# Ordering the mixers and attentions of a two-layer trunk with busy intervals for ScalarE and VectorE

## The chip, the cores and the metric

The kernel runs on one core of a Trainium2 chip. The metric is the device time of one execution in microseconds (us). The kernel before took 1425.7 us, the median of three runs from 1424.77 to 1426.21.

Five engines work in parallel, each taking its own instructions strictly in order: TensorE (PE in the profile: matmuls; PEld: the loads of their stationary operand), VectorE (DVE), ScalarE (ACT), GpSimd (POOL) and SyncE (SP, which here only issues transfers). An instruction that has to wait holds up all that stand behind it on its engine.

## The reference

A trunk of two layers over 512 positions of width 1024, with a memory of 256 positions, all in float32:

```
x += mixer(rms_norm(x));  x += cross_attention(rms_norm(x), mem);  x += conv_ffn(rms_norm(x))    (twice)
layer 0 mixer: forgetting attention, 8 heads of 64  |  differential attention, 4 heads (2 x 64, values 128)
    fox:   softmax(q k' / 8 + F_q - F_k, causal) v,  F = cumsum(log_sigmoid(gate))
    diff:  (softmax(q1 k1' / 8) - lam * softmax(q2 k2' / 8)) v, then an rms_norm of its own
layer 1 mixer: mLSTM, 4 heads (q, k 128 after a causal convolution, values 256), gated, normalised
conv_ffn: gated, with a depthwise convolution of 3 taps and 2816 hidden columns
```

## The kernel before, in words

**Precision.** Every weight arrives by a transfer of 512 KB that SP issues (`weight`, L325) and is split in two: ScalarE rounds it to the fast matmul type (`wh`, a CAST), VectorE computes the rest (`wl`, a TENSOR_TENSOR). A product is three matmuls: high by high, low by high, high by low (`mm3`, L340 to L342; with tokens on the partitions L402 to L404). So TensorE carries three passes of everything, and a projection of 1024 by 128 columns for 512 positions is 24 matmuls of 512 columns.

**Stages.** Mixer 0 runs from 0 to about 230 us of the span, cross attention 0 to about 375, the FFN of layer 0 to about 720, mixer 1 to about 915, cross attention 1 to about 1080, and the FFN of layer 1 with the final norm to the end. The FFNs are ordered by another scheduler (`Sched`), which the change leaves alone.

**What sets the order.** Mixers and cross attentions are a list of items (`Plan.add`): a piece of TensorE work with a planned duration, what it depends on, a priority, the buffers it takes and frees, and a `chain` of what follows on other engines, such as 0.6 us on D (VectorE) and then 0.52 on A (ScalarE). `Plan.run` walks a planned TensorE clock, and each time takes the item with the best priority that can start now. When it takes an item, the Python function of the item is called, and that writes the instructions of all engines into the program: the order of VectorE's, ScalarE's and GpSimd's instructions follows from the order in which items are taken. Planned times are used for nothing else; on the chip, semaphores decide.

Four banks (`acc`) hold the sums of projections, two banks (`s`) the scores, two (`w`) transposes, weighted values and the like. Helpers record most VectorE and ScalarE instructions under one line, L262.

**Softmax.** A score is two matmuls (L750, L751) into an `s` bank; VectorE adds the bias or mask and takes the minimum in one instruction (CUSTOM_DVE_ANT_0), ScalarE takes the exponential with its sum (ACTIVATE x<-x,sm), VectorE inverts the sum (RECIPROCAL) and scales (TENSOR_SCALAR). Then TensorE transposes (L781), VectorE and ScalarE copy the result out (`pt`), and TensorE multiplies by the values: a weigh (L793 for a differential head, L1008 for a pair of fox heads).

**Roots.** A differential head's rms_norm (`p_far_norm`) goes: TensorE sums squares by columns (L499), VectorE makes `z`, GpSimd takes the power (`y`, L507) and issues two transfers, `roots` out to DRAM (L448) and `hrb` back, spread to all partitions (L452); then VectorE multiplies the head by it (`ta<-ta,warm,hrb`, a SCALAR_TENSOR_TENSOR). There is one `hrb` buffer. The heads of the mLSTM do the same (`num<-num,vec,hrb`).

**Fillers.** In mixer 0 the keys of cross attention 0, `acc<-mem` with 256 columns and 192 matmuls in all, stand at the lowest priority (`p_fill`), and so does the output projection (`p_out`, its weights `wo`). Whatever is free at that moment fills TensorE where the attention has nothing ready.

**mLSTM.** The gates (`p_gate`) go through a long run of small VectorE and ScalarE instructions; `ucols` (L1630) transposes their result back. Meanwhile q and k of the first head are projected, convolved on VectorE (`hs`, `cv`) and ScalarE, and scored (L1721, `s<-q,k`).

## Time and profile before

| | us |
|---|---|
| median of three runs | 1425.7 |
| lowest, highest | 1424.77, 1426.21 |
| the profiled execution's own time | 1423.48 |
| its span in the trace | 1421.7 |
| TensorE busy | 1403.3 (99%) |
| VectorE busy | 1133.5 (80%) |
| ScalarE busy | 823.8 (58%) |
| GpSimd busy | 129.9 (9%) |

The profiled execution is 2.2 us below the median of the runs. Time that the profile calls busy isn't always time at full rate: a matmul of 512 columns lasts 0.38 us in the trace and a new one starts every 0.216 us, so the starts tell more than the shares. The granted clock (PEclk) says for each slice of the span at what part of full speed TensorE's clock ran; 1.00 is full speed.

### The profile page before, as it was taken

The page shows a single profiled execution, that of the slowest core. Times are in us where ns is not written, and L with a number is a line of the kernel's source. Part 1 is how long each engine was busy: PE and PEld are TensorE (multiplying, and loading weights), DVE is VectorE, ACT ScalarE, POOL GpSimd, SP SyncE. Part 2 cuts the span into 40 slices and gives each one's busy share as a digit, 9 for nine tenths or more (in the row PEclk, how much of TensorE's full clock was granted, in tenths as well). Part 3 has the DMA queues.
Part 4 walks back from the last instruction along what each step waited for, and adds up shares of the span by engine and source line. Part 5 has one row for each costly group of instructions (what it writes and reads, how often), then busy time and mean ns, then how long its engine had stood idle before and what let it go on. Part 6 is the DMA issues. An engine that isn't in the chain of part 4 may idle for free.

```text
span 1421.7 us, 22241 instructions
## 1 busy us (share of the span) xinstructions
PE 1403.3 (99%) x8440; PEld 1262.9 (89%) x8440; DVE 1133.5 (80%) x1906; ACT 823.8 (58%) x1382; POOL 129.9 (9%) x189
## 2 busy tenths in 40 slices
PE   9999999999999999999999999999999999999998
PEld 7878788899889999999887788989988999999997
DVE  7778596666689999999768657667667999999984
ACT  7777574444476656566456654445445665656655
POOL 0001240000001111110001210000000111111000
PEclk9999999999999999999999999999999999999999
DMA  5233224323248777773233322323323886777522
GB/s 205 90 108 108 90 79 152 132 76 133 86 150 217 191 180 184 182 182 106 86 105 112 105 95 97 119 92 120 130 74 120 212 202 171 193 179 185 143 77 80
DMA packets 69211, 190.02 MB, mean 134 GB/s; under 512 B 7552, under 2 KB 7552, under 8 KB 69104
## 3 DMA queue, kind: packets, MB, share of 16 engines
q1 hardware_dynamic: 55648, 153.48, 32.3%
q0 software_dynamic: 12448, 34.00, 13.7%
q8 instruction: 66, 1.08, 0.3%
q10 hardware_dynamic: 1008, 1.12, 0.2%
q14 instruction: 41, 0.34, 0.1%
HBM read 186.43 MB, written 2.15 MB: 133 GB/s over the span
## 4 chain that ended last, share of the span: by engine, by line
PE 83%; DVE 8%; ACT 4%; issue 3%; DMA 1%; POOL 1%; SPq 0%; POOLq 0%; DVEq 0%; ACTq 0%
PE acc L340 16%; PE acc L341 16%; PE acc L342 16%; PE w L340 5%; PE w L342 5%; PE w L341 5%; PE s L340 3%; PE s L341 3%; PE s L342 3%; PE acc L402 2%; PE acc L404 2%; PE acc L403 2%; DVE wl L262 2%; DVE x L262 1%; PE w L1765 1%
## 5 line engine op out<-in xcount | busy, mean ns | idle before, releaser
L262 ACT CAST wh<-raw 128x1024 fp32r<-128x1024 f32 (+2 forms) x229 | 235.0, 1027 | 205.6 <-PE acc L341 118.8
L262 DVE TENSOR_TENSOR wl<-raw,wh 128x1024 fp32r<-128x1024 f32 (+2 forms) x229 | 274.2, 1198 | 38.7 <-ACT wh L262 38.2
L340 PE MATMUL acc<-xh,wh 128*128 128x512 f32 (+1 forms) x800 | 278.6, 348 | 0.8 <-ACT v L262 0.8
L341 PE MATMUL acc<-xl,wh 128*128 128x512 f32 (+1 forms) x800 | 274.0, 343 | 0.0
L342 PE MATMUL acc<-xh,wl 128*128 128x512 f32 (+1 forms) x800 | 273.6, 342 | 0.0
L340 PEld LDWEIGHTS acc<-xh,wh 128*128 128x128 f32 x800 | 152.5, 191 | 14.5 <-ACT v L262 1.2
L342 PEld LDWEIGHTS acc<-xh,wl 128*128 128x128 f32 x800 | 152.4, 190 | 13.9
L341 PEld LDWEIGHTS acc<-xl,wh 128*128 128x128 f32 x800 | 152.5, 191 | 13.2
L262 DVE SCALAR_TENSOR_TENSOR c<-hs,vec,c 128x512 f32<-128x512 f32 x176 | 131.8, 749 | 3.8 <-ACT c L262 0.8
L340 PE MATMUL w<-ah,wh 128*128 128x512 f32 x304 | 115.7, 381 | 0.2 <-ACT c L262 0.2
L342 PE MATMUL w<-ah,wl 128*128 128x512 f32 x304 | 115.2, 379 | 0.0
L341 PE MATMUL w<-al,wh 128*128 128x512 f32 x304 | 115.2, 379 | 0.0
L262 ACT ACTIVATE c<-hs,vec 128x512 f32<-128x512 f32 x88 | 70.8, 811 | 9.9 <-DVE hs L262 5.4
L262 ACT CAST ah<-c 128x512 fp32r<-128x512 f32 x44 | 27.2, 619 | 83.8 <-DVE c L262 83.8
L262 DVE TENSOR_TENSOR x<-acc,x 128x512 f32<-128x512 f32 (+1 forms) x43 | 28.1, 653 | 54.2 <-PE acc L342 53.4
L340 PEld LDWEIGHTS w<-ah,wh 128*128 128x128 f32 x304 | 57.6, 190 | 8.0 <-DVE x L262 0.9
L342 PEld LDWEIGHTS w<-ah,wl 128*128 128x128 f32 x304 | 57.5, 189 | 8.1
L341 PEld LDWEIGHTS w<-al,wh 128*128 128x128 f32 x304 | 57.6, 190 | 6.5
L342 PE MATMUL acc<-mem,wl 128*128 128x256 f32 (+1 forms) x192 | 59.9, 312 | 0.0
L340 PE MATMUL acc<-mem,wh 128*128 128x256 f32 (+1 forms) x192 | 59.6, 311 | 0.0
L341 PE MATMUL acc<-mem,wh 128*128 128x256 f32 (+1 forms) x192 | 59.6, 311 | 0.0
L1446 POOL DMA_DIRECT2D sa<-in_up_dram x36 | 30.8, 857 | 290.6 <-DMA sa<-in_up_dram 212.7
(357 smaller groups left out, 3750.5 us busy)
## 6 DMA issues: line engine op xcount, KB each, us to landing
raw<-in_up_dram SPq DMA_DIRECT2D x52, 512.0 KB, 3.7
sa<-in_up_dram SPq DMA_DIRECT2D x36, 512.0 KB, 3.4
sa<-in_up_dram POOLq DMA_DIRECT2D x36, 512.0 KB, 5.9
raw<-in_down_dram SPq DMA_DIRECT2D x32, 512.0 KB, 3.6
ra<-in_up_dram SPq DMA_DIRECT2D x36, 256.0 KB, 4.0
sb<-in_up_dram POOLq DMA_DIRECT2D x36, 256.0 KB, 4.9
raw<-in_xk_dram SPq DMA_DIRECT2D x16, 512.0 KB, 3.2
raw<-in_wo_dram SPq DMA_DIRECT2D x16, 512.0 KB, 3.3
```

The costliest lines, as they stand in the source:

```text
L262: i = issue(*a, **k)
L340: mm(out, wh, xh, start=first, stop=False, skip_group_check=parts)
L341: mm(out, wh, xl, start=False, stop=False, skip_group_check=parts)
L342: mm(out, wl, xh, start=False, stop=last, skip_group_check=parts)
L402: mm(ps, xh[k][:, ts], wh, start=(k == 0), stop=False)
L403: mm(ps, xh[k][:, ts], wl, start=False, stop=False)
L404: mm(ps, xl[k][:, ts], wh, start=False, stop=(k == 7))
L1446: return add("POOL", 0.0029 * cols, lambda: nc.gpsimd.dma_start(out(), src(), accum_op=ALU.add), deps, due, (), (), 6.0)
L1765: nc.tensor.matmul(ps[:, lo:], vv[s][:, c], a[:], start=(s == 0), stop=(s == 3))
```

## The change

No instruction of the computation is added or taken away. What changes is the planner and its numbers, and by them the order of the instructions.

- **Busy intervals.** For A (ScalarE), D (VectorE) and G (GpSimd) the planner kept one time each: when the engine is free. Now it keeps a list of busy intervals, and `place` puts a piece of work into the first gap that holds it. A long chain that waits for something no longer pushes all later work behind it in the plan.
- **Costs.** Planned durations change: ScalarE's 0.52 and 0.5 become 0.6, an exponential 0.4 + 0.45 for 512 columns instead of 0.3 + 0.4, GpSimd's power 1.3 instead of 1.05, and so on. The values' evacuation counts on ScalarE alone (`rest=False`). The gate chain of mixer 1 becomes a delay of 14 us with a load spread over gaps, and the step after it 4.0 instead of 2.7.
- **Banks.** An `acc` bank of a projection is planned free at the end of the first step of its chain (`soon`), the first read, and no longer at the end of all.
- **Holding.** An item that waits for a buffer kept every later item off this buffer; now only if it could start within 2.5 us (`HOLD`).
- **Roots and memory.** `LATE`, the planned time between asking for the roots and using them, is 15 us instead of 12, so the use is written later. The memory's transfers are planned 16 instead of 10 us ahead of use.

```diff
-ROW_DMA, SPREAD_DMA, LATE = 2.7, 6.0, 12.0
+ROW_DMA, SPREAD_DMA, LATE = 2.7, 6.0, 15.0
+HOLD = 2.5
...
+        def place(e, at, d):
+            b = eng[e]
+            while b and b[0][1] < t - 8.0:
+                b.pop(0)
+            n = 0
+            for n, (x, y) in enumerate(b):
+                if at + d <= x:
+                    break
+                at = max(at, y)
+            else:
+                n = len(b)
+            b.insert(n, (at, at + d))
+            return at + d
...
-                held |= set(i.take)
-                if any(len(self.res[r]) < i.take.count(r) for r in i.take):
+                if any(len(res[r]) < i.take.count(r) for r in i.take):
+                    held |= set(i.take)
                     continue
...
+                if at < t + HOLD:
+                    held |= set(i.take)
...
             for e, d in pick.pre:
-                eng[e] = max(eng[e], t - 4.0) + d
+                place(e, t - 4.0, d)
             t += pick.dur
             u = t + (0.1 if pick.chain else 0.0)
+            clear = None
             for e, d in pick.chain:
-                if e == "-":
-                    u += d
-                    continue
-                u = max(u, eng[e]) + d
-                eng[e] = u
-                u += 0.06
+                u = u + d if e == "-" else place(e, u, d) + 0.1
+                clear = clear or u
             for e, d in pick.load:
-                eng[e] = max(eng[e], t) + d
+                while d > 0.0:
+                    place(e, t, min(d, 0.6))
+                    d -= 0.6
...
-                    self.banks[pick.st["banks"].pop(0)] = u
+                    banks[owned.setdefault(id(pick.st), list(pick.st.get("banks", ()))).pop(0)] = clear if pick.soon else u
...
-            last = pl.add(lambda c=c: load(c), 0, (), 0, after=at + step * c - 10.0, order=[*order, last])
+            last = pl.add(lambda c=c: load(c), 0, (), 0, after=at + step * c - 16.0, order=[*order, last])
...
-            g = pl.add(lambda: None, 0, [g], 1, chain=(("A", 1.0), ("D", 7.0), ("A", 0.5)))
-            gk = pl.add(lambda: None, 0, [g], 2, chain=(("-", ROW_DMA),))
+            g = pl.add(lambda: None, 0, [g], 1, chain=(("-", 14.0),), load=(("A", 5.0), ("D", 7.0)))
+            gk = pl.add(lambda: None, 0, [g], 2, chain=(("-", 4.0),), load=(("A", 2.4), ("D", 1.2)))
```

In the rows below, numbers behind a name tell tiles of one kind apart; they differ between the two kernels. L262 before is L295 after, and all later lines move by 33.

**A root's use, mixer 0, third differential head.** On TensorE before, the sums of squares of that head stand here, between two projections of the fox part, in front of the last transposes of the head behind (`w_1489`) and two scores:

```order
L340 MATMUL acc_276_1409<-xh_32_234,wh_1404 128x512
L341 MATMUL acc_276_1409<-xl_33_235,wh_1404 128x512
L342 MATMUL acc_276_1409<-xh_32_234,wl_1405 128x512
L499 MATMUL s_1480<-ones_82,tb_1422 128x2 x4
L781 MATMUL w_1489<-ident,x_141 128x128 x4
L750 MATMUL s_1500<-ka_257_1331,qa_249_1285 128x384
```

On VectorE before, the use of its root (`hrb_1568`) stands in the middle of the softmax of the next scores; `x_138` and `x_142` are scores, `pt` copies of transposes:

```order
L262 TENSOR_SCALAR x_140<-x_140,sm_1507 128x384
L262 COPY pt_1370<-w_1543 128x128
L262 ISA x_142,sm_1557<-s_1550,tb_1551 128x384
L262 ISA sm_1557 128x1
L262 SCALAR_TENSOR_TENSOR ta_1421<-ta_1421,warm,hrb_1568 128x512
L262 ISA x_138,sm_1566<-s_1559,tb_1560 128x512
L262 ISA sm_1566 128x1
L262 RECIPROCAL sm_1557<-sm_1557 128x1
L262 TENSOR_TENSOR ml_135<-ta_1421,mh_129 128x512
L262 TENSOR_SCALAR x_142<-x_142,sm_1557 128x384
L262 COPY pt_1466<-w_1582 128x128
```

On TensorE after, the sums of the second and third head stand together inside a projection, before the first fox scores:

```order
L375 MATMUL acc_244_1263<-xh_19_193,wl_1259 128x512
L814 MATMUL w_1281<-ident,x_137 128x128 x4
L532 MATMUL s_1288<-ones_82,tb_1242 128x2 x4
L532 MATMUL s_1297<-ones_82,tb_1251 128x2 x4
L373 MATMUL acc_244_1263<-xh_25_215,wh_1258 128x512
```

On VectorE after, the use of the third head's root (`hrb_1359`) stands behind eight scores of the first fox pair, the second's (`hrb_1351`) 44 rows ahead of it:

```order
L295 ISA x_138,sm_1558<-s_1551,tb_1552 128x512
L295 ISA sm_1558 128x1
L295 TENSOR_TENSOR kb_115<-tmp_1518,ka_302_1520 64x512
L295 ISA x_137,sm_1567<-s_1560,tb_1561 128x512
L295 ISA sm_1567 128x1
L295 TENSOR_TENSOR kb_117<-tmp_1518,ka_303_1524 64x512
L295 SCALAR_TENSOR_TENSOR ta_1250<-ta_1250,warm,hrb_1359 128x512
L295 COPY pt_1406<-w_1578 128x128
```

Between sums and use there were, on TensorE, six matmuls of a projection, a weigh, and a few transposes and scores; now there are almost two projections and the scores of a pair.

**The end of mixer 0.** On TensorE before, behind the last weigh (`w_2425`) stand matmuls of an output block (`acc_518`) on heads that are long done (`mh`, `ml`), before the first one that reads the weigh's result (`qa_509`):

```order
L1008 MATMUL w_2425<-pt_2213,v_1213 64x128
L342 MATMUL acc_518_2489<-mh_129,wl_2485 128x512
L340 MATMUL acc_518_2489<-mh_130,wh_2484 128x512
L341 MATMUL acc_518_2489<-ml_136,wh_2484 128x512
L342 MATMUL acc_518_2489<-mh_130,wl_2485 128x512
L340 MATMUL acc_514_2456<-qa_509_2434,wh_2451 128x512
```

On TensorE after, three output blocks are done up to their last part by then. The last scores, the last transposes (`w_2363` to `w_2392`, 16 in a row), the weigh (`w_2399`) and the three blocks' last parts, which read its result (`qa_507`, `qa_508`), follow each other, and only then the cross attention's keys (`acc<-mem`):

```order
L814 MATMUL w_2392<-ident,x_137 128x128 x4
L1041 MATMUL w_2399<-pt_2143,v_1228 64x512
L1041 MATMUL w_2399<-pt_2339,v_1228 64x512
L1041 MATMUL w_2399<-pt_2143,v_1230 64x384
L1041 MATMUL w_2399<-pt_2339,v_1230 64x384
L1041 MATMUL w_2399<-pt_2143,v_1232 64x256
L1041 MATMUL w_2399<-pt_2339,v_1232 64x256
L1041 MATMUL w_2399<-pt_2143,v_1234 64x128
L1041 MATMUL w_2399<-pt_2339,v_1234 64x128
L373 MATMUL acc_408_1965<-qa_507_2408,wh_1960 128x512
L373 MATMUL acc_424_2011<-qa_507_2408,wh_2006 128x512
L373 MATMUL acc_435_2052<-qa_507_2408,wh_2047 128x512
```

What filled the wait behind the weigh, matmuls on other data, is gone from this place.

**The first head of the mLSTM.** On TensorE before, `ucols` stands ahead of the first projection of q:

```order
L404 MATMUL acc_1465_7884<-wh_8037,xl_1453_7836 128x512
L1630 MATMUL s_8074<-ident,cv_7961 128x4 x4
L340 MATMUL acc_1508_8087<-xh_1415_7636,wh_8082 128x512
L341 MATMUL acc_1508_8087<-xl_1416_7637,wh_8082 128x512
L342 MATMUL acc_1508_8087<-xh_1415_7636,wl_8083 128x512
```

On TensorE after, it stands 42 matmuls later, inside the second projection. The first score (`s_8249<-q,k`) keeps its place, 87 rows behind the old one of `ucols`, in the same row of both orders:

```order
L375 MATMUL acc_1514_8124<-xh_1445_7791,wl_8120 128x512
L1663 MATMUL s_8143<-ident,cv_7961 128x4 x4
L373 MATMUL acc_1514_8124<-xh_1449_7818,wh_8119 128x512
L374 MATMUL acc_1514_8124<-xl_1450_7819,wh_8119 128x512
L375 MATMUL acc_1514_8124<-xh_1449_7818,wl_8120 128x512
```

The orders of VectorE and ScalarE up to that first score are the same in both kernels but for single rows. In the FFNs nothing moves.

119 lines of the change are left out of this document (66 added, 53 removed).

## The prediction

> **What bounds the kernel now.** I read the page's busy shares first, then windows of 20 us, then TensorE's waits, then the timeline around each wait.
>
> ```profile
> PE 1403.3 (99%) x8440; PEld 1262.9 (89%) x8440; DVE 1133.5 (80%) x1906; ACT 823.8 (58%) x1382; POOL 129.9 (9%) x189
> ```
>
> TensorE is the bound everywhere, and the change takes no matmul away. Only what TensorE waits can be won: 1421.7 - 1403.3 = 18 us of idle time at most, plus whatever hides inside "busy". The windows say where it lies (columns: length, then busy us and instructions of PE, PEld, DVE, ACT, POOL, then the granted clock).
>
> ```profile
> 100.00:120.00 20.00, 19.01 (x106) 16.07 (x105) 12.16 (x44) 16.50 (x40) 4.42 (x7) 1.00 0.22 70
> 140.00:160.00 20.00, 17.50 (x88) 14.86 (x88) 13.74 (x35) 12.32 (x27) 9.33 (x13) 0.91 0.31 93
> 180.00:200.00 20.00, 18.55 (x136) 16.02 (x136) 19.21 (x65) 15.86 (x39) 9.11 (x15) 1.00 0.19 63
> 300.00:320.00 20.00, 20.00 (x110) 17.81 (x110) 12.84 (x27) 8.87 (x19) 0.00 (x0) 1.00 0.23 79
> ...
> 740.00:760.00 20.00, 18.53 (x89) 15.97 (x88) 13.63 (x18) 14.87 (x19) 1.13 (x2) 1.00 0.25 79
> 760.00:780.00 20.00, 19.06 (x87) 15.86 (x86) 17.80 (x26) 12.65 (x22) 4.64 (x10) 1.00 0.39 124
> 780.00:800.00 20.00, 19.15 (x83) 14.59 (x82) 14.63 (x29) 12.98 (x22) 5.18 (x9) 1.00 0.49 154
> ```
>
> Cross attention (300 to 320) has nothing to give: 20.00 of 20. The two mixers have. One window, 140 to 160, also shows a clock of 0.91. TensorE's waits, longest first (us in total, times, longest):
>
> ```profile
> PE w L781 <- DVE pt L262: 2.5, 1, 2.5
> PE s L1721 <- ACT k L262: 1.8, 2, 0.9
> PE s L1630 <- DVE cv L262: 1.5, 1, 1.5
> PE acc L609 <- DVE ones L262: 1.1, 1, 1.1
> PE w L793 <- ACT pt L262: 1.0, 1, 1.0
> PE w L781 <- DVE sm L262: 0.9, 1, 0.9
> PE s L750 <- DVE sm L262: 0.9, 2, 0.7
> ```
>
> These 9.7 us are single places, not a shortage of engines, so order can cure them. The 1.1 is the start of the program and stays.
>
> **Roots further ahead.** The 2.5 us is this (timeline: start, length):
>
> ```profile
> 148.46 0.55 POOL L452 DMA_DIRECT2D hrb<-roots  x1 [2.05 <-DMA roots<-y]
> ...
> 151.81 0.95 PE L499 MATMUL s<-ones,tb 128*128 128x2 f32 x8
> 152.19 0.75 DVE L262 SCALAR_TENSOR_TENSOR ta<-ta,warm,hrb 128x512 f32<-128x512 f32 x1 [2.06 <-DMA hrb<-roots]
> ...
> 155.26 0.69 PE L781 MATMUL w<-ident,x 128*128 128x128 f32 x2 [2.50 <-DVE pt L262]
> ...
> 157.02 0.63 PE L341 MATMUL acc<-xl,wh 128*128 128x512 f32 x1
> 157.45 0.63 PE L342 MATMUL acc<-xh,wl 128*128 128x512 f32 x1
> ...
> 158.72 0.38 PE L342 MATMUL acc<-xh,wl 128*128 128x512 f32 x1
> 158.93 0.38 PE L340 MATMUL acc<-xh,wh 128*128 128x512 f32 x1
> ```
>
> The spread root was issued at 148.46 and landed at about 152.1. VectorE stood 2.06 us in front of it with the softmax of the waiting scores behind it; TensorE ran dry for 2.50. Then matmuls start 0.43 us apart instead of 0.21, until 158.7: half clock for 158.7 - 155.3 = 3.4 us, which loses half of that, 1.7. The window agrees: 9% of 20 us is 1.8 us of granted clock. So this one root costs 2.5 + 1.7 = 4.2 us. After the change, sums and use lie two projections and a pair's scores apart: 48 matmuls by 0.216 are over 10 us, and the scores come on top. What a root needs: GpSimd's power (third number: 1265 ns), two issues of 0.55, and two landings:
>
> ```profile
> L507 POOL TENSOR_TENSOR y<-z,power 128x4 f32<-128x4 f32 x4 | 5.1, 1265 | 18.5 <-DVE z L262 18.5
> ...
> hrb<-roots POOLq DMA_DIRECT2D x7, 256.0 KB, 3.6
> ...
> roots<-y POOLq DMA_DIRECT2D x7, 2.0 KB, 2.0
> ```
>
> Together 1.3 + 1.1 + 2.0 + 3.6 = about 8 us; a margin is left. On GpSimd's queue the third head's spread now stands behind the second's, and its single buffer is free only when VectorE has read that: until then it holds up the bias selections (`tb`) of the next scores behind it. VectorE's read is 44 rows ahead of the next use, some ten microseconds, and selections are wanted later than that; I cost it at nothing. Term: **-4.2**.
>
> **Keys ahead of scores, weighs behind their turns.** Two more places of mixer 0 (the first with TensorE's rows around the kb that it needed):
>
> ```profile
> 130.90 1.40 DVE L262 TENSOR_TENSOR kb<-tmp,ka 64x512 fp32r<-64x512 f32 x2
> ...
> 131.23 0.27 PE L750 MATMUL s<-ka,qa 128*128 128x256 f32 x1
> 131.63 0.38 PE L751 MATMUL s<-kb,qa 128*128 128x256 f32 x1
> ...
> 132.36 0.38 PE L751 MATMUL s<-kb,qa 128*128 128x256 f32 x1
> ```
>
> Four matmuls of 256 columns (131.23 to 132.36 are the first and the last; 0.11 us each where nothing is waited for, half of the 0.216 of 512 columns) take 1.34 us from 131.23 to 132.57: 0.9 lost, though all is "busy". In the new order the first pair's keys are done 6.5 us of matmuls before its first score, against 3.9 here (counted in the order by 0.216 us): -0.9. The weigh at 104.4 that waited 1.0 for ScalarE's `pt` came late because ScalarE had waited 2.91 for the memory:
>
> ```profile
> 98.53 0.42 ACT L262 ACTIVATE sq<-raw 128x256 f32<-128x256 f32 x1 [2.91 <-DMA raw<-in_mem_dram]
> ...
> 104.38 1.12 PE L793 MATMUL w<-pt,v 128*128 128x512 f32 x2 [0.99 <-ACT pt L262]
> ```
>
> The memory's transfer is planned 6 us earlier, but in SP's queue it still stands behind three weight transfers and takes the buffer of the first of these, so by my count it is issued only as that buffer comes free, and ScalarE waits nearly as long. The two weighs of that place, however, now stand 14 us of matmuls behind the copies they need. What ScalarE is late for next is the values' evacuation that frees the bank for the following projection; with the durations of its rows I find it done 0.7 us in time. Term -1.0. The wait of 0.7 at a score (last row of the waits) falls in a cluster of scores that is broken up: -0.7. Together: **-2.6**.
>
> **New tight places in mixer 0.** The same kind of count, row durations strung along each engine's new order, finds two. Early in the differential heads eight scores stand within 4.8 us of matmuls, and VectorE's last part before the transposes behind them comes out 0.7 us late: between 0 and 1.5, I take +0.7. The end of the mixer is worse. There TensorE has nothing but the last pair's transposes, its weigh, and the output parts that read the weigh. VectorE works off what remains of the softmax (groups of instructions of one shape, with the sum in us and the mean in ns behind the bar):
>
> ```profile
> L262 DVE CUSTOM_DVE_ANT_0 x<-s,tb 128x512 f32<-128x512 f32 x8 | 5.4, 675 | 1.0 <-PE s L751 1.0
> ...
> L262 DVE TENSOR_SCALAR x<-x,sm 128x384 f32<-128x384 f32 x8 | 3.6, 456 | 0.0
> ...
> L262 DVE COPY pt<-w 128x384 f32<-128x384 f32 x9 | 4.9, 549 | 0.9 <-PE w L781 0.9
> ...
> L262 DVE TENSOR_TENSOR kb<-tmp,ka 64x512 fp32r<-64x512 f32 x10 | 6.9, 692 | 0.4 <-ACT ka L262 0.2
> ...
> L262 ACT CAST qa<-tmp 64x512 fp32r<-64x512 f32 x10 | 6.1, 613 | 1.2 <-PE s L751 1.1
> ```
>
> Stringing such rows (at most 0.68 for each of the last scores, 0.69 for a difference between them, about 0.46 for each of four scalings, 0.55 twice for copies) I get 1.4 us of waiting in the transposes, 1.0 at the weigh, and 0.9 behind it, where the 0.61 of `qa` on ScalarE and its difference on VectorE stand between the weigh and its reader: +3.3. Before, the mixer's last stretch lost 20 - 18.55 = 1.4. Lower end: a weigh's result alone, 0.6 + 0.9 = 1.5; upper end 5. Net: **+1.9**. For places that I did not string up I add **+1.0** (0 to 4), since the new order of about 190 us has as many chances of a short wait as the old, which had five.
>
> **Mixer 1.** The gate chain on VectorE and ScalarE is as long as before and in the same order, so what it ends in comes at the same time:
>
> ```profile
> 769.44 0.38 PE L342 MATMUL acc<-xh,wl 128*128 128x512 f32 x1
> ...
> 770.09 0.61 ACT L262 ACTIVATE k<-cv 128x512 f32<-128x512 f32 x1
> ...
> 770.75 1.45 PE L1721 MATMUL s<-q,k 128*128 128x512 f32 x3 [0.94 <-ACT k L262]
> ```
>
> With `ucols` moved back its wait of 1.5 goes; TensorE arrives at the first score 1.5 us earlier, at about 768.1 instead of 769.66, and still finds k only at 770.7. The wait moves there: 0.94 becomes about 2.6, a loss equal to the gain. The second head's score (0.9 of the 1.8) now stands behind 9.6 us of matmuls instead of 8.1 after its k; its wait falls to about 0.2. Net **-0.6**.
>
> A gap of 2.6 us at one place is as long as the one at 152.8 to 155.3, after which the clock was halved. If this one halves it too, 1.7 us are lost again; the other waits here, up to 1.5, show no halving (clock 1.00 from 740 to 800). I count it as a rival. The Trainium skill, "TensorE: Matmul & The Clock Gate", Part 1, has the clock fall after an idle window of about 3.4 us, and its section on oscillation warns of idle gaps over about 3.4 us; by it a gap of 2.6 would cost nothing more. The trace here shows a halving after 2.5, so the measurement speaks against the figure as a limit, while its 3.4 us as the length of a stay agrees with 155.3 to 158.7.
>
> **Cross attentions and the rest.** Their order changes in places, but with 20.00 of 20 busy they can only lose: +0.2. Start of the program and FFNs: same order, 0.
>
> **The sum.** -4.2 - 2.6 + 1.9 + 0.7 + 1.0 - 0.6 + 0.2 = -3.6. Against the profiled execution, 1423.5, that is 1419.9; it ran 2.2 under the median of the runs, so the median to expect is 1425.7 - 3.6 = **1422.1**. A measurement of this kernel can tell about 0.2% (2.85 us) from no change: below 1422.85 is faster, above 1428.55 slower.
>
> **The rivals.**
> - *The larger gain.* The tail costs no more than its lower end (-1.8 against my sum), nothing is lost where I did not look (-1.0), and the cluster of eight scores costs nothing (-0.7): 1418.6, down to 1416 if ucols' wait doesn't move (-1.5 or more). For it: ScalarE and VectorE are 58% and 80% busy, and each wait of before had one late instruction as its cause.
> - *The waits only move (no change).* The gap at the mLSTM's first score halves the clock (+1.7) and the unseen places cost their upper half (+2 to +3): 1424 to 1427. For it: two of the three waits of mixer 1 are moved, not removed, and mixer 0's end has lost its fillers. That the change should do nothing because TensorE is 99% busy belongs here too; against it stands that 4.2 us hang on one transfer.
> - *Slower: the end of mixer 0 bound by VectorE.* From 180 to 200 VectorE was busy 19.21 of 20 already. The fillers that TensorE had there are now output blocks used up earlier, and behind the last transposes each microsecond that VectorE is behind costs one. One pair's softmax is about 9 us of VectorE (an estimate from the rows above: eight scores at about 0.5 for the minimum, 0.46 for the scaling and 0.2 for what lies between). If VectorE enters the last pair a whole pair behind, the tail costs 3.3 + 9 and the sum turns to 1431; it decides from 6.5 us of backlog on. Against it: by my count VectorE is abreast there within 1.5 us, and before, at the same load, the wait was 0.9.
>
> **How the numbers follow.** Forecast, 1419 to 1422.85: 0.38. Larger gain, below 1419: 0.17. Waits only move, 1422.85 to 1428.55: 0.27. Slower: 0.18. Faster is 0.38 + 0.17 = 0.55, same 0.27, slower 0.18. The forecast's own range is 1419 to 1425. For 8 in 10 the range takes in the larger gain down to 1416 and the slower case up to 1429.5, which leaves out some 0.04 below and 0.15 above.
>
> **What would show it.** Right: no half clock between 120 and 165, no idle time of VectorE on `hrb` in mixer 0, TensorE's starts 0.11 us apart at the first fox scores, the weighs of differential heads without a wait; `ucols` without a wait and a wait of 2 to 3 us on `k` at the first L1754; and waits on `pt`, `sm` or `qa` of 1.5 to 5 us in all between 185 and 200. Wrong: a new wait above 2 us elsewhere in mixer 0, a wait of ScalarE on the memory that TensorE feels, or waits inside the cross attentions.

## The result, and the profile after

The changed kernel took 1429.7 us (median of 6 runs, 1428.64 to 1430.89) against 1424.6 for the kernel before in runs beside it (6 runs). The ratio is 1.0034, with a 95% interval of 1.0024 to 1.0044: slower by a third of a per cent, where 1422.1 was forecast. The first line of the page of after, against 1403.3 us for TensorE before:

```profile
PE 1405.6 (98%) x8440; PEld 1261.6 (88%) x8440; DVE 1132.3 (79%) x1906; ACT 824.2 (58%) x1382; POOL 129.3 (9%) x189
```

The work is the same. Where the 5 us lie is told best by one instruction that both kernels have: the first matmul behind FFN 0's second wait for `c`. It parts the span into layer 0 (ahead of it) and layer 1 (it and what follows). TensorE's timeline has it here, first before, then after:

```profile
687.02 0.45 PE L340 MATMUL w<-ah,wh 128*128 128x512 f32 x1 [0.15 <-ACT c L262]
```

```profile
687.48 0.45 PE L373 MATMUL w<-ah,wh 128*128 128x512 f32 x1 [0.15 <-ACT c L295]
```

Layer 0 takes 0.5 us more, and layer 1 takes 1428.1 - 687.48 = 740.6 instead of 1421.7 - 687.02 = 734.7, so 5.9 more. Of these, 0.8 are a wait for a weight's transfer at the start of FFN 1 (last section). In the tables below, layer 1 is worked out in this way for each run, from its own profile. The windows of after that answer those shown before (busy of PE, PEld, DVE, ACT, POOL, then clock):

```profile
100.00:120.00 20.00, 19.65 (x91) 15.87 (x90) 15.31 (x35) 17.54 (x34) 2.13 (x4) 1.00 0.33 89
140.00:160.00 20.00, 18.01 (x90) 14.77 (x90) 18.93 (x55) 15.19 (x35) 5.33 (x10) 1.00 0.33 107
180.00:200.00 20.00, 18.62 (x102) 14.16 (x101) 17.37 (x62) 13.10 (x36) 7.26 (x15) 1.00 0.14 41
200.00:220.00 20.00, 17.36 (x100) 12.23 (x100) 11.76 (x37) 9.69 (x22) 1.42 (x3) 1.00 0.33 105
300.00:320.00 20.00, 20.00 (x114) 17.95 (x113) 13.31 (x29) 9.01 (x20) 0.00 (x0) 1.00 0.27 91
740.00:760.00 20.00, 20.00 (x96) 17.28 (x95) 13.53 (x18) 15.23 (x20) 1.10 (x2) 1.00 0.22 70
760.00:780.00 20.00, 17.55 (x80) 14.51 (x79) 18.77 (x29) 12.79 (x23) 4.82 (x10) 1.00 0.44 129
780.00:800.00 20.00, 19.75 (x91) 15.39 (x90) 13.96 (x28) 12.48 (x20) 5.23 (x9) 1.00 0.48 150
800.00:820.00 20.00, 17.21 (x71) 13.35 (x71) 14.79 (x22) 11.44 (x17) 4.61 (x8) 0.91 0.27 88
860.00:880.00 20.00, 18.65 (x85) 15.50 (x84) 15.03 (x22) 8.64 (x13) 1.33 (x4) 1.00 0.32 93
```

The half clock has left 140 to 160 and stands in 800 to 820. There, and from 860 to 880, TensorE had no idle time before:

```profile
800.00:820.00 20.00, 20.00 (x98) 16.67 (x98) 13.84 (x21) 12.38 (x17) 5.10 (x9) 1.00 0.23 67
860.00:880.00 20.00, 20.00 (x92) 16.89 (x91) 16.91 (x26) 9.91 (x15) 0.79 (x3) 1.00 0.30 105
```

TensorE's waits after (us in total, times, longest):

```profile
PE s L1754 <- ACT k L295: 3.8, 2, 2.4
PE s L532 <- DVE hsq L295: 3.0, 2, 2.8
PE s L783 <- DVE sm L295: 2.0, 2, 1.7
PE s L783 <- ACT memrb L295: 1.4, 1, 1.4
PE acc L375 <- DVE wl L295: 1.1, 1, 1.1
```

The long wait for a root, 2.5 us in mixer 0, is gone. In its place stand a wait for the mLSTM's first score (2.4), which was forecast, and one for the squares of its second head (`hsq`, 2.8), which was not. The latter in TensorE's timeline, with the first and the last of the slow matmuls behind it:

```profile
813.67 1.05 PE L532 MATMUL s<-ones,hsq 128*128 128x2 f32 x8 [2.79 <-DVE hsq L295]
...
815.29 0.63 PE L437 MATMUL acc<-wh,xl 128*128 128x512 f32 x1
...
817.43 0.63 PE L436 MATMUL acc<-wl,xh 128*128 128x512 f32 x1
```

Matmuls start 0.43 us apart there, half clock, which costs another 1.7 us. In the same place of after, VectorE and then ScalarE:

```profile
802.08 0.69 DVE L295 SCALAR_TENSOR_TENSOR emt<-emt,hsq 128x512 f32<-128x512 f32 x1 [3.42 <-ACT hsq L295]
...
804.60 0.75 DVE L295 SCALAR_TENSOR_TENSOR cv<-hs,vec,cv 128x512 f32<-128x512 f32 x1
806.02 0.75 DVE L295 SCALAR_TENSOR_TENSOR num<-num,vec,hrb 128x512 f32<-128x512 f32 x1 [0.67 <-DMA hrb<-roots]
806.69 0.74 DVE L295 SCALAR_TENSOR_TENSOR cv<-hs,vec,cv 128x512 f32<-128x512 f32 x1
807.35 0.74 DVE L295 SCALAR_TENSOR_TENSOR num<-num,vec,hrb 128x512 f32<-128x512 f32 x1
808.02 0.74 DVE L295 SCALAR_TENSOR_TENSOR cv<-hs,vec,cv 128x512 f32<-128x512 f32 x1
...
812.93 0.69 DVE L295 TENSOR_TENSOR hsq<-hsq,th 128x512 f32<-128x512 f32 x1 [0.81 <-ACT th L295]
```

```profile
800.85 0.72 ACT L295 ACTIVATE mk<-mk,ucol 128x512 f32<-128x512 f32 x1 [3.91 <-POOL mk L1748]
801.47 0.58 ACT L295 ACTIVATE hsq<-w 128x512 f32<-128x512 f32 x1
...
808.79 0.63 ACT L295 ACTIVATE th<-cv 128x512 f32<-128x512 f32 x1 [3.33 <-DVE cv L295]
809.33 1.13 ACT L295 ACTIVATE th<-num 128x512 f32<-128x512 f32 x1
```

VectorE multiplies the first head by its root (`num<-num,vec,hrb`) in between the taps of the third head's convolution (`cv`). ScalarE stands 3.33 us for these taps, with the second head's `th` behind, from which `hsq` comes. Earlier it stood 3.91 us for the third head's mask (`mk`), with the second head's denominators (`hsq<-w`) behind. Most of that time cost nothing: the product that the denominators read ended on TensorE only at 799.93 + 0.81 = 800.74, so the mask held them for about 0.7 us.

```profile
799.93 0.81 PE L1777 MATMUL w<-mk,ones 128*128 128x384 f32 x2
```

From denominators to the last square pass 813.62 - 801.47 = 12.1 us. Before, this way took 802.75 to 810.01, 7.3 us, and the use of the first head's root came only behind it, at 813.77 (timelines of before, ScalarE and then VectorE):

```profile
802.75 0.60 ACT L262 ACTIVATE hsq<-w 128x512 f32<-128x512 f32 x1 [0.62 <-PE s L499]
```

```profile
809.32 0.69 DVE L262 TENSOR_TENSOR hsq<-hsq,th 128x512 f32<-128x512 f32 x1 [1.40 <-ACT th L262]
...
813.77 1.42 DVE L262 SCALAR_TENSOR_TENSOR num<-num,vec,hrb 128x512 f32<-128x512 f32 x2 [1.76 <-DMA hrb<-roots]
```

### The profile page after: what moved, and what is told of

It reads as the page before. It is cut to its first block, busy times and chain, and to the rows that moved or that the text cites. A ratio compares the mean times of both kernels' runs of the same rounds, so it can differ in the third digit from the quotient of the medians.

```text
span 1428.1 us, 22234 instructions
## 1 busy us (share of the span) xinstructions
PE 1405.6 (98%) x8440; PEld 1261.6 (88%) x8440; DVE 1132.3 (79%) x1906; ACT 824.2 (58%) x1382; POOL 129.3 (9%) x189
## 4 chain that ended last, share of the span: by engine, by line
PE 81%; DVE 7%; ACT 6%; DMA 3%; issue 3%; POOL 1%; POOLq 0%; SPq 0%; DVEq 0%; ACTq 0%
PE acc L373 16%; PE acc L374 16%; PE acc L375 16%; PE w L373 5%; PE w L374 5%; PE w L375 5%; PE s L374 3%; PE s L375 3%; PE s L373 3%; PE acc L435 2%; PE acc L436 2%; PE acc L437 2%; DVE wl L295 1%; ACT wh L295 1%; ACT x L295 1%
## 5 line engine op out<-in xcount | busy, mean ns | idle before, releaser
L295 ACT CAST wh<-raw 128x1024 fp32r<-128x1024 f32 (+2 forms) x229 | 235.0, 1027 | 227.8 <-PE acc L374 116.9
L295 DVE TENSOR_TENSOR wl<-raw,wh 128x1024 fp32r<-128x1024 f32 (+2 forms) x229 | 274.2, 1199 | 46.8 <-ACT wh L295 46.3
L295 DVE SCALAR_TENSOR_TENSOR c<-hs,vec,c 128x512 f32<-128x512 f32 x176 | 131.8, 749 | 3.8 <-ACT c L295 0.8
L295 ACT ACTIVATE c<-hs,vec 128x512 f32<-128x512 f32 x88 | 70.9, 812 | 10.7 <-DVE hs L295 6.2
L295 ACT CAST ah<-c 128x512 fp32r<-128x512 f32 x44 | 27.2, 619 | 84.1 <-DVE c L295 84.1
L295 DVE TENSOR_TENSOR x<-acc,x 128x512 f32<-128x512 f32 (+1 forms) x43 | 28.0, 653 | 56.5 <-PE acc L375 56.5
```

The costliest lines, as they stand in the source:

```text
L295: i = issue(*a, **k)
```

## The experiments

**Which layer: one planner for each.** The planner and its numbers of before stand beside the changed ones, and each layer uses one of them.

```diff
+                self.__class__ = OldBuilder if layer in (1,) else Builder      # e1; (0,) in e2
```

> Layer 0 (mixer and cross attention) is ordered as after the change, layer 1 as before it, each with its own planner and numbers. Theory A (the loss lies in mixer 1: from the starts of TensorE's matmuls I count 5.2 us more waiting between 740 and 900 us than before, and about 0.3 us more in mixer 0): about 1424.5 us, within 1.5 us of the kernel before. Theory B (mixer 0 loses as well, hidden in work that the profile calls busy): 1427 us or more.

> The other half: layer 0 ordered as before the change, layer 1 as after it. Theory A: 1429 to 1431 us, with the wait of 2.8 us for the squares of the second mLSTM head (hsq) and the half clock behind it again in the trace. Theory B: clearly less than 1429.

| | median, us | ratio to before, 95% interval | layer 1, us |
|---|---|---|---|
| layer 1 as before (e1) | 1425.14 | 0.9998 [0.9988, 1.0008] | 734.7 |
| layer 0 as before (e2) | 1430.15 | 1.0036 [1.0024, 1.0049] | 738.6 |

The whole loss comes from layer 1. Layer 0 gains nothing and loses nothing that these runs can tell (e1's interval is 1.4 us to each side), although its 4.2 us at the root are gone. The last column, here and below, comes from one profiled execution of each kernel and says where time lies; whether a kernel is faster is read from the medians.

**Two numbers of mixer 1 undone.** The planned gate chain (e3), and the distance of the root's use (e4):

```diff
-            g = pl.add(lambda: None, 0, [g], 1, chain=(("-", 14.0),), load=(("A", 5.0), ("D", 7.0)))
+            g = pl.add(lambda: None, 0, [g], 1, chain=(("A", 1.0), ("D", 7.0), ("A", 0.5)))
...
-ROW_DMA, SPREAD_DMA, LATE = 2.7, 6.0, 15.0
+ROW_DMA, SPREAD_DMA, LATE = 2.7, 6.0, 12.0
```

> The changed kernel with one part undone: the gate chain of mixer 1 counts on the engines again (1.0, 7.0 and 0.5 us, then 2.7) and is no delay of 14 us with a load. Theory C (the late gate chain moves the work of the first heads together, and that makes the wait at the second head's sums): mixer 1 loses its 5.2 us and the time is about 1425. Theory D (the wait comes from where the first head's root stands among the second head's and the third head's work, whatever the gates): the wait at ucols (1.5 us) is back, the wait for hsq stays, and the time is 1428 to 1431.

> The changed kernel with the roots' planned distance back at 12 us. If the longer distance makes the wait of mixer 1 (theory E), the wait for hsq goes and the time falls by 3 to 5 us, to 1425 to 1427, unless the wait for a root in mixer 0 comes back (4.2 us with its half clock), which would eat that. If the intervals alone make it (theory F), it stays at 1428 or more.

e3: 1429.47, ratio 1.0031 [1.0017, 1.0044], layer 1 740.4. e4: 1431.17, 1.0040 [1.0029, 1.0050], layer 1 742.4. Neither is the cause. In e3 the wait for `hsq` was 1.54 us; the wait at `ucols`, which was expected back, did not come, and the first score waited 2.90. With `LATE` back at 12, TensorE's order in mixer 1 stays as it is in the changed kernel, and the wait for `hsq` was 2.5 us.

**Away with the first head's root, or sums put off.** e5 doesn't multiply the mLSTM's first head by its root and gain, so that part of the normalisation is left out. e6 plans the sums of the mLSTM's roots 8 us later. e8 does that and plans the memory's preparation in mixer 0 wider apart (`MEM_STEP` 46 instead of 24). e7 is the kernel before with the new planner alone, all numbers old.

```diff
+                        if h == 0:
+                            continue                                            # e5, in scaled
...
-  scaled, ns, p + 3, fdeps=oe, ...
+  scaled, [pl.add(lambda: None, 0, ns, p + 3, chain=(("-", 8.0),))], p + 3, fdeps=oe, ...      # e6, e8
```

> The changed kernel, but the first mLSTM head isn't multiplied by its root and its gain (two instructions of 0.74 us on VectorE and the wait for hrb ahead of them are left out, so that head's result isn't normalised). Theory G (the first head's root, used between the taps of the third head's q convolution, delays the tanh that ScalarE has in front of the second head's squares): the wait for hsq at the second head's sums falls from 2.8 us to under 0.7, the half clock behind it goes, and the time falls by 3.5 to 5 us, to about 1425. Theory H (the squares are late because VectorE stood 3.4 us in front of the minimum with the denominator, and ScalarE's mask of a later head stood in front of that): the wait stays at 2 us or more, and the time at 1428 to 1430.

> The changed kernel with the sums of squares of each mLSTM head planned 8 us later, and so its root's use; nothing is left out. On VectorE the first head's root then stands behind the second head's squares and behind the third head's q convolution, and on GpSimd the power stands behind the next masks. Theory G: wait and half clock go, 1424.5 to 1426 us. Theory H: 1428 or more, unless the denominator's minimum, which also moves behind the convolution's first taps, is what counted.

> The kernel before with the new planner alone (busy intervals, holding within 2.5 us, banks free at their first read), and all planned costs and distances as before. If the intervals as such bring the loss (theory F of the run on LATE), 1428 us or more. If it is the raised costs that put the items where they are, about 1425 or less.

> As the kernel with the later sums, and the second half of the memory is prepared 46 instead of 24 us behind the first, in layer 0. Its four pairs of instructions then no longer stand in front of the first fox scores on VectorE. The wait of 1.7 us there (and 0.5 behind it) should fall by the 1.3 us that these instructions take, if nothing else is late; against the kernel with the later sums 1 us or so less. Theory: if the wait is VectorE's whole queue there, which also holds the next pair's q and its weights, it falls only by these 1.3; if it goes as a whole, the memory alone made it.

| | median, us | ratio, 95% interval | layer 1, us | wait for the second head's `hsq` |
|---|---|---|---|---|
| no use of the first root (e5) | 1432.56 | 1.0051 [1.0038, 1.0064] | 741.1 | 3.27 |
| sums 8 us later (e6) | 1431.16 | 1.0040 [1.0024, 1.0055] | 743.5 | none |
| planner alone (e7) | 1430.86 | 1.0039 [1.0026, 1.0052] | 736.5 | 0.08 |
| sums and memory later (e8) | 1430.36 | 1.0038 [1.0025, 1.0050] | 739.4 | none |

Three things follow. First, with the sums put off the wait goes, but scores then wait for products on VectorE (`at`), 3.0 us in all, 2.8 of them for one of the last head's in e6. The profiled execution of e6 is its slowest, 5.2 us above its median, and 2.54 us of its layer 1 are a wait at the start of FFN 1. In e8, where the memory's preparation comes later, the first fox score no longer waits its 1.66 us, but later scores and transposes wait 0.57 and 1.62 for `sm`, so as much is lost there.

Second, the planner alone loses as much in all, but elsewhere: layer 1 takes 736.5, while layer 0 takes 6.3 us more than before (693.29 - 687.02). By these profiles the new numbers mend the planner's mixer 0 and spoil its mixer 1; e10 below tests the second half. Third, without the first head's use the wait did not go, which spoke against the theory that VectorE's queue makes it. The trace of e5 reads otherwise. From the denominators to the last square pass 816.43 - 806.34 = 10.1 us, 2.0 less than in the changed kernel, but the denominators come late. VectorE, GpSimd and then ScalarE of e5:

```profile
801.24 0.68 DVE L295 TENSOR_TENSOR mixed<-num,mixed 128x512 fp32r<-128x512 f32 x1
...
802.04 0.69 DVE L295 TENSOR_TENSOR num<-num,sg 128x512 f32<-128x512 f32 x1
...
815.74 0.69 DVE L295 TENSOR_TENSOR hsq<-hsq,th 128x512 f32<-128x512 f32 x1 [1.22 <-ACT th L295]
```

```profile
801.21 2.42 POOL L540 TENSOR_TENSOR y<-z,power 128x4 f32<-128x4 f32 x1 [2.75 <-DVE z L295]
```

```profile
805.21 0.72 ACT L295 ACTIVATE mk<-mk,ucol 128x512 f32<-128x512 f32 x1 [5.29 <-POOL mk L1748]
805.83 0.60 ACT L295 CAST mixed<-num 128x512 fp32r<-128x512 f32 x1
806.34 0.59 ACT L295 ACTIVATE hsq<-w 128x512 f32<-128x512 f32 x1
```

The power of the first head's root took 2.42 us on GpSimd, against 1.04 in the changed kernel's profile. Beside it VectorE runs `mixed` and `num` products that in the changed kernel stand behind the use of the root. The third head's mask came behind the power, and ScalarE held the second head's denominators behind that mask until 806.34. So e5 shortened VectorE's queue and lengthened the other by the same edit, and its time says nothing against VectorE's.

**That queue alone, and the mLSTM's numbers.** e9 pins the exponentials of a head's first two masks so that they are recorded behind the denominators of the head in front. e10 gives the mLSTM mixer its old numbers under the new planner, and e11 only the old durations of a convolution's chain.

```diff
+                        if s < 2:
+                            nc.scalar.follow()
                         nc.scalar.activation(mk[:, :n], mk[:, :n], AF.Exp, scale=-1.0, ...      # e9
...
-            cc = (("D", 0.6), ("A", 0.7), ("D", 2.3), ("A", 0.7), ("D", 0.66), ("A", 0.6))
+            cc = (("D", 0.6), ("A", 0.52), ("D", 1.98), ("A", 0.52), ("D", 0.66), ("A", 0.52))  # e10, e11
```

> The changed kernel, with ScalarE's exponential of the first two masks of each head of the mLSTM mixer pinned ahead of their own scores' products only, so that the framework orders it later: on ScalarE the third head's masks then stand behind the second head's denominators, not in front of them. Theory M (the wait of 2.8 us at the second head's sums comes from ScalarE standing 3.9 us for the third head's mask, which GpSimd makes behind the first head's root, with the denominators queued behind): that wait falls below 1 us, the half clock behind it goes, lost time of TensorE between 740 and 900 us falls from 9.4 to about 5, median 1425 to 1426. Rival W (the waits of this mixer only move): the wait goes or shrinks, others grow by as much, lost time stays at 8 to 10.5, median 1429 to 1431. Theory G (VectorE's queue with the first head's use of its root) is already weak, since the wait stayed where that use was left out: by it nothing changes.

> The changed kernel, with the mLSTM mixer's own numbers as before (gate, convolution, gate columns, rows, denominators, products, last step, values), new planner and all other new numbers kept. Theory N (the loss in mixer 1 is in the numbers given to the new planner, not in the planner itself; with old numbers its mixer 1 lost 5.2 us): lost time between 740 and 900 us about 5.2, mixer 0 as in the changed kernel (8.8), median 1425 to 1426.5. Rival W (any new order of this mixer costs about the same): lost time 8 to 10.5 there, median 1429 to 1431.

> The changed kernel, with only the planned times of a convolution's chain of steps as before (0.6, 0.52, 1.98, 0.52, 0.66, 0.52 instead of 0.6, 0.7, 2.3, 0.7, 0.66, 0.6 us). Theory N1 (this one number is what spoils mixer 1): lost time between 740 and 900 us 5 to 6, median 1425 to 1426.5. Theory N without N1: 7 to 10.5, median over 1428.

| | median, us | ratio, 95% interval | layer 1, us | wait for `hsq` |
|---|---|---|---|---|
| masks behind (e9) | 1432.27 | 1.0043 [1.0031, 1.0055] | 742.0 | 3.82 |
| mLSTM's numbers old (e10) | 1429.03 | 1.0024 [1.0012, 1.0035] | 739.4 | 1.30 |
| convolution's numbers old (e11) | 1429.73 | 1.0029 [1.0015, 1.0042] | 742.2 | 1.26 |

The theory of the masks alone fell too, and so did that of the convolution's numbers alone (e11). In e9 the denominators no longer stood behind a mask (801.85; ScalarE waited for TensorE's product), but VectorE stood 2.33 us for the root in the midst of the taps. VectorE, then ScalarE of e9:

```profile
808.14 0.75 DVE L295 SCALAR_TENSOR_TENSOR num<-num,vec,hrb 128x512 f32<-128x512 f32 x1 [2.33 <-DMA hrb<-roots]
```

```profile
801.85 0.60 ACT L295 ACTIVATE hsq<-w 128x512 f32<-128x512 f32 x1 [3.85 <-PE w L1779]
...
810.92 0.64 ACT L295 ACTIVATE th<-cv 128x512 f32<-128x512 f32 x1 [4.38 <-DVE cv L295]
```

The theory that the mLSTM's numbers alone make the loss did not hold either: e10 came out at 1429.0, not at 1425 to 1426.5. It has almost the order of e7 on TensorE in mixer 1, and yet its layer 1 took 2.9 us more. What differs in the traces is again this place: the power took 2.30 us in e10 and 1.05 in e7, so that roots and masks came later. VectorE and GpSimd of e10:

```profile
791.52 1.22 DVE L295 TENSOR_TENSOR wl<-raw,wh 128x1024 fp32r<-128x1024 f32 x1
```

```profile
791.69 2.30 POOL L540 TENSOR_TENSOR y<-z,power 128x4 f32<-128x4 f32 x1 [2.72 <-DVE z L295]
```

In e10 a weight's `wl` runs on VectorE beside the power; in e7 it had ended before. It is not the chance of one execution: e11, with the same rows there, has 2.30 too. But no run changes this alone.

**Both queues.** e12 ties the first head's use of its root behind the second head's squares, with an order on VectorE alone, and the computation stays whole. e13 does that and keeps the masks behind the denominators as in e9.

```diff
+                        if (h, d) == (1, 1):
+                            behind["ins"] = nc.vector.last                       # the second head's last square
...
-                        nc.vector.scalar_tensor_tensor(out=nm[:], in0=nm[:], scalar=self.col("hn", 2 * h + d), in1=rb[:], ...
+                        i = nc.vector.scalar_tensor_tensor(out=nm[:], in0=nm[:], scalar=self.col("hn", 2 * h + d), in1=rb[:], ...
+                        if h == 0 and "ins" in behind:
+                            nc.vector.tc.add_manual_dep(i.ins, behind["ins"], nc.vector.info, reason="use behind squares")
```

> The changed kernel, with the first head's use of its root on VectorE tied behind the second head's squares (an order alone; the computation is whole). TensorE's order is as in the changed kernel but for the second head's sums, which stand three matmuls (0.65 us) earlier. Theory T (two queues delay the second head's squares, each enough for most of the wait: VectorE with the first head's use of its root between the third head's taps, ScalarE with the third head's masks in front of the second head's denominators): the taps end some 2.1 us earlier, since 2 x 0.75 us of use and 0.67 us of waiting leave their midst; the wait of 2.8 us becomes 0.7 plus 0.65, so 1 to 1.5 us, if GpSimd's power takes 1.0 us as there, and more if it takes 2.3 us. Half clock may stay. Median 1426.5 to 1428.5. Rival W (whatever is mended here comes back at other places of the mixer): 1429 to 1431.

> Both at once: the first head's use of its root behind the second head's squares, and the exponentials of the third head's first masks behind the second head's denominators. Theory T: the wait at the second head's sums falls below 1 us, with no half clock behind it; layer 1 (from the second FFN's wait for c at about 687 us on) takes 735 to 737 us instead of 741, median 1425 to 1426.5. Rival W: the wait goes, others in the mixer grow by as much, layer 1 stays at 739 us or more, median 1429 to 1431.

| | median, us | ratio, 95% interval | layer 1, us | wait for `hsq` |
|---|---|---|---|---|
| use behind (e12) | 1426.87 | 1.0010 [1.0000, 1.0019] | 737.2 | 0.80 |
| use and masks behind (e13) | 1426.28 | 1.0009 [1.0000, 1.0019] | 736.8 | 0.44 |

On TensorE the order stays but for the second head's sums, which stand three matmuls earlier. The wait fell, and no new one of its size came in its place. The squares of e13 on VectorE, with the taps together and the use behind:

```profile
805.33 2.33 DVE L295 SCALAR_TENSOR_TENSOR cv<-hs,vec,cv 128x512 f32<-128x512 f32 x3
...
811.33 0.69 DVE L295 TENSOR_TENSOR hsq<-hsq,th 128x512 f32<-128x512 f32 x1 [1.26 <-ACT th L295]
811.94 1.41 DVE L295 SCALAR_TENSOR_TENSOR num<-num,vec,hrb 128x512 f32<-128x512 f32 x2
```

and two windows of TensorE in e13 (length, busy, clock):

```profile
760.00:780.00 20.00, 17.55 (x72) 0.91 0.42 133
...
800.00:820.00 20.00, 19.56 (x91) 1.00 0.29 84
```

The window from 800 has its clock back. The use of the root in VectorE's queue is the cause that these runs show: with e12 alone, whose edit orders nothing else, the wait falls from 2.79 to 0.80 us, the half clock behind it goes, and the ratio falls from 1.0034 [1.0024, 1.0044] to 1.0010. That the masks add anything is not shown. Between the traces of e12 and e13 the denominators come 0.4 us earlier and the wait is 0.36 shorter, but the medians can't tell the two apart, and masks behind without the use behind (e9) brought nothing. (Of the 3.4 us by which layer 1 is shorter in e12's profile, 0.8 are the wait at the start of FFN 1, which e12 lacks; against that, e12 has half clock behind the first score, some 1.7, which the changed kernel's profile lacks.) What is left over before in layer 1, 736.8 against 734.7, is the first score's wait with a half clock behind it (the window from 760), and the last head's first score (1.44); that is read from the trace, not tested.

**A version that beats both.** In the tail of mixer 0 the first weights of the filling products (`wl`, the wait of 1.1 above) were made behind the last head's `qa`, since they were planned from 210 us on. e14 is e13 with fills from 170 us on. e16 has these fills and the changed planner in layer 0, and layer 1 as before. e15 is the kernel before, profiled again.

```diff
-FILLS, FILL_AT, FILL_PRIO = 2, (210.0, 140.0), 99
+FILLS, FILL_AT, FILL_PRIO = 2, (170.0, 140.0), 99
```

> As the run with both, and the memory products that fill mixer 0 allowed from 170 us on instead of 210, so that their first weights are made before the last head's keys and values queue in front of them. Theory: the wait of 1.1 us at the fills (218 us) goes and the fills come into the stalls of 182 and 208 to 215 us, so 1 to 3 us less than that run. Rival: they take buffers of weights and VectorE's time from the last head, and as much is lost there.

> The kernel before, profiled once more: it tells which of the small differences between traces are those of an execution. If the waits of 0.3 to 2.5 us at the start of the FFNs (445 and 1138 us) belong to the executions and not to the change, they may show here too; mixers as in the first profile.

> A version meant to beat both: layer 0 by the changed planner and numbers, with its filling memory products allowed from 170 us on; layer 1 by the planner and numbers of before. By adding stages: layer 0 ran to its second FFN wait for c at 685.6 us where fills may start at 170 (with 1.5 us of FFN wait in it), against 686.5 and 687.3 before; layer 1 by the old planner took 735.2 to 735.5 us. So 1421 span and 1422 to 1424 median, 1 to 3 us under the kernel before. Rival: the changed tail of layer 0 gives it back in the cross attention behind it, same as before (1425).

| | median, us | ratio, 95% interval | layer 0, layer 1, us |
|---|---|---|---|
| e13 with fills from 170 (e14) | 1424.06 | 0.9991 [0.9982, 1.0001] | 686.1, 738.8 |
| before, again (e15) | 1424.58 (one run) | | 687.9, 734.9 |
| layer 0 new with fills, layer 1 old (e16) | 1423.38 | 0.9979 [0.9968, 0.9990] | 685.3, 735.2 |

e16 is faster than the kernel before by 0.2%, the only one of these. So layer 0's change can gain some 2 us, which the changed kernel gave back at the late fills: where fills may start at 170, the stretch from 180 to 200 is busy 19.53 of 20 in e14 instead of 18.62, with the `memrb` wait gone. Both pairs that differ in this number alone agree: from e1 to e16 the ratio falls by 0.0019, from e13 to e14 by 0.0018. The two profiles of before differ by 0.9 us in layer 0 and 0.3 in layer 1. Others are further from their medians (e14's by 2.6 us), so differences of a microsecond or two between single profiles prove nothing by themselves. (In e14's layer 1, 0.9 is the wait at the start of FFN 1, and the last head's first score waited 2.1 with a half clock behind it.)

## Why the prediction was wrong

**The root (-4.2): right.** From 140 to 160 the clock is 1.00 instead of 0.91, and the use of the third head's root no longer waits. Part of it was not in the count: before, GpSimd's power of that root took 1.96 us (143.55, beside a `wl` on VectorE), and in the changed kernel 1.04. The root's spread stood 7.5 us on GpSimd's queue for the single buffer, as was foreseen, and TensorE did not feel it.

**Keys, weighs, scores (-2.6): right at their places.** The wait for `pt` and the slow first fox scores are gone; the wait of 0.7 at a score shrank to 0.44, for `z`. But the first fox scores then met the next item.

**The cluster of eight scores (+0.7): small,** 0.17 at the transposes behind them. **Cross attentions (+0.2):** 20.00 of 20 busy again from 300 to 320.

**Places not strung up (+1.0, 0 to 4): too small.** Three of them alone cost 4.5 us: the first fox scores wait 1.66 and 0.33 for `sm`, since VectorE (18.93 of 20 busy from 140) has a weight's `wl`, two `qa` and the memory's preparation in its queue ahead of the minimum. A score waits 1.38 for `memrb`, behind three conversions on ScalarE. The fills wait 1.10 for `wl`. With the tail this makes layer 0 a zero instead of -3.2.

**The tail (+3.3): the right kind, oversized.** The waits of its transposes, weigh and `qa` are 0.13, 0.20, 0.43 and 0.67, 1.4 us in all, near the lower end of 1.5. The slower rival, a tail bound by VectorE, did not occur.

**Mixer 1 (-0.6): here the prediction failed.** Layer 1 takes 5.9 us more, 0.8 of them at FFN 1, and e1 and e2 put the whole loss there. What the prediction strung up came true: `ucols` without a wait, the first score with one of 2.45 where 2.6 was forecast, the second head's score no longer late. It stopped there, as if the gate chain were all that this mixer's order had changed. Behind it the new order had brought the first head's root (sums, GpSimd's power, use) and the third head's masks ahead of the second head's squares: 2.8 us of waiting, 1.7 of half clock. The last head's score waits another 1.35. The step that failed is the term for the rest of this mixer, which was put at nothing without being strung up. What was missing there is what the prediction itself did for mixer 0's root: to ask what stands behind a waiting instruction on its engine. e12 shows that it counts: with the use moved behind those squares, the ratio falls to 1.0010.

**The half clock as a rival** was put at the right cause and the wrong place: not at the first score's 2.45 in this profile, but at the sums. Five other kernels with the same wait at that score do have half clock behind it (last section), so by these runs it was luck that it stayed away here.

One sentence about the kernel before was too simple. The order of VectorE's, ScalarE's and GpSimd's instructions does not follow from the order of items alone: in the mixers the framework orders them once more, and only those that are pinned stay behind the one recorded before them. e9 and e12 move rows on VectorE and ScalarE by a pin or a tie, without a change of the plan.

## What to carry to other kernels

When an order brings a chain forward, look at every engine that the chain crosses for whose work now stands behind its waits: here the use of the first head's root stood between the third head's taps on VectorE, and so, through ScalarE, the second head's squares came late. Leaving an instruction out also moves what stood behind it, and that can lengthen another queue (e5); moving it, with everything kept (e12), is the cleaner test, so look at the trace before a theory is dropped. And a change that gains in one stage and loses in another is worth splitting by stage: half of this one, with one number put right, beats the kernel before.

## What the runs showed of the hardware

**Half clock after short waits.** The wait for `hsq` stands in front of eight matmuls of two columns (1.05 us), and 1.30 us of it sufficed. TensorE in e10, with the first and the last of the slow matmuls:

```profile
809.90 1.05 PE L532 MATMUL s<-ones,hsq 128*128 128x2 f32 x8 [1.30 <-DVE hsq L295]
...
811.81 0.63 PE L374 MATMUL acc<-xl,wh 128*128 128x512 f32 x1
...
814.37 0.63 PE L374 MATMUL acc<-xl,wh 128*128 128x512 f32 x1
```

In front of these sums waits of 1.26, 1.30, 1.54, 2.03, 2.50, 2.79, 3.27 and 3.82 us were all followed by a stay at half clock, those of 0.80, 0.50 and 0.44 by none. Before full matmuls the outcome varied: the first mLSTM score waited 2.45 to 2.47 us in the profiles of ten kernels, and the clock from 760 to 780 was 1.00 in five of them (the changed kernel among them) and 0.91 in five (e13 among them). So a wait's length alone does not decide it, and no run here separates what else does. The Trainium skill, "TensorE: Matmul & The Clock Gate", Part 1, has the clock fall after an idle window of about 3.4 us. Most stays at half clock behind these sums are of that length here (811.8 to 815.2 in e10), and those of e4 and e9 of twice that (clock 0.89 from 800 to 820 and 0.94 from 820 to 840, together 6.8 us). But the gaps that led to them were as short as 1.26 us, with 1.05 us of narrow matmuls behind.

**GpSimd's power of 128 x 4 elements** took between 1.03 and 2.42 us for a head's root. The time goes with the order and not with the execution: it was 1.96 and 1.95 in the two profiles of before (third differential head), 2.30 in both e10 and e11, 1.35 in each of e9, e13 and e14 (first mLSTM head). All that took 1.35 us or more ran beside at least 0.7 us of VectorE instructions that combine two tiles of which neither is a matmul bank (`wl<-raw,wh`, `num<-num,sg`, `mk<-mk,at`). Not each such neighbour lengthens it (1.06 beside 0.69 us of `cv<-th,cv` in before, at 806.11), and no run tests it.

**FFN starts:** a wait for a weight's transfer (`u`, 0.2 to 2.5 us) showed at one or both FFN starts in 13 of the 16 profiles with any part of the new planner, not in e10, e13 and e16, and in neither profile of before. In e2 it showed in the layer of the old order. Whether it belongs to the change stays open.
